# Norms of Q and K by a GpSimd power, in a written order, and idle products at the start of an encoder block

## The chip, the core and the metric

The kernel runs on one core of one Trainium2 chip. The metric is the device time of one execution in microseconds (us). A core has TensorE for matrix products (PE; its weight loads are PEld), VectorE (DVE), ScalarE (ACT), GpSimd (POOL) and SyncE (SP), which issues most of the transfers. Each works through its own instructions in order. Products land in PSUM, in eight banks of 128 x 512 float32; everything else works in SBUF.

## What is computed

One layer of a bidirectional encoder on 1024 tokens of width 1024. The part that matters:

```
u = RMSNorm(x)
[q|k|v|cB|cC|cH|gA|gB] = u @ W_in            # q, k, v: 512 wide each, 8 heads x 64
q = rms_norm(q per head, q_norm_g);  k = rms_norm(k per head, k_norm_g)
y_A = neighbourhood_attention(q, k, v) @ W_A;  y_B = cB * conv3(cC * cH) @ W_B
x = x + (sigmoid(gA) * y_A + sigmoid(gB) * y_B) @ W_o
x = x + relu(RMSNorm(x) @ W1)^2 @ W2
rms_norm(z) = z * rsqrt(mean(z^2) + 1e-6) * g
```

## The kernel before

Every product is made of float16 parts: each operand is scaled by a power of two and split into a high part and a low part, and three passes (high x high, high x low, low x high; `PASSES`, L453) are summed in PSUM. The high part is a ScalarE copy to float16, the low part a VectorE subtraction.

**The start, to V.** Rows come in eight blocks of 128. For blocks 0 and 1, V's columns are multiplied in float32: `native_turn` (L570) transposes the raw rows on TensorE and ScalarE (VectorE for part of block 1) copies them out, `native` (L581) multiplies them by the raw weights. `native(0, 0, lower)` and `native(0, 0, upper)` are two halves of the first product. Meanwhile `largest` and `v_largest` find the largest weight, a matmul with the ones tile (`v_sum`, L546) brings it to all partitions, and `v_part` splits V's weights. The norms of the rows use `rpow` (L417): a scale and a power of -1/2 on GpSimd, on one column per block. The other six blocks go through float16 and transposing DMAs (`ln_turn`) and then through `v_unit` (L528), 24 matmuls of 128x512, in the order 2, 6, 3, 7, 4, 5.

**Weights.** A `Chunk` is one weight matrix piece: `prep` (L255) squares its raw pieces on ScalarE, sums over partitions by a matmul with the ones tile (`all_sum`, L200), derives the scale on VectorE (L426 to L433, L279) and splits it (L306 high, L297 low). These steps are a generator; `push` puts it in the background list and `tick` advances it. `apart(units[0], n)` makes it wait for n further units of TensorE. Five raw buffers are filled by SP as they come free.

**The forms.** Pairs of row blocks (n, n + 4) are scaled (`sform_rows`, ScalarE), combined (`sform_sums`, four GpSimd additions of 128x512), split (L504 ScalarE, L506 VectorE, 128x2048) and stored to DRAM for the gates much later. The foreground generator `sforms` does this at marks counted in units (`SFORM`), and ScalarE issues the stores.

**Q and K.** Sixteen units follow, Q's eight blocks and then K's, each 24 matmuls into one bank of 128 tokens x 512. `unit` (L207) issues the matmuls, runs what is due behind the unit before, and then gives the foreground some steps and the background some ticks. Behind each unit stands a foreground generator `qk_vec` (L711): ScalarE copies the bank out with the scale, squares the copy; VectorE sums per head; `rstd` (L401) takes the square root on ScalarE and refines its reciprocal by five small VectorE steps; VectorE multiplies, ScalarE and VectorE split; `finish_qk` (L740) turns the block by a transposing DMA three units later. Generators of several blocks interleave, one step each per round. Two bank tags, "d" and "o", alternate. After Q the code flushes what the background still has of K's parts, after K what it has of the first convolution's.

**After that** two convolution units (`ch_mms`, 24 matmuls each) run, then attention (L936 onward), in which scores, convolution and softmax are interleaved by a written order; then gates and branches, the output projection, and the MLP, mostly 12-matmul units.

Of the kernel before, what the change touches and what calls it, by code (L numbers as in the profile page):

```python
# [52 lines left out]
def encoder_block(ctx: ExitStack, tc: tile.TileContext, x, weights, cols, gqk, rel, masks, out):  # L53
# [25 lines left out]
    sc = base.tile([128, 516], F32, name="sc")  # L79
    sci = sc.bitcast(I32)  # L80
    area = {"keep": [0, 0, 148], "prep": [148, 148, 244], "tmp": [244, 244, 516]}
# [163 lines left out]
    class Chunk:  # L245
# [9 lines left out]
        def prep(self):  # L255
# [5 lines left out]
            if self.kind in "QKCG":  # L261
                self.parts = wsp.tile([128, 2, tot], F16, name="w16_ws", tag="ws")
                for p, (k, w) in enumerate(self.widths):
                    while len(self.raw) <= p:
                        yield WAIT
                    A.activation(self.parts[:, 1, :k * w].bitcast(BF16), self.raw[p][:, :k * w], AF.Square,
                                 accum_out=sc[:, at(rm, p)])
                    spend(0, 300 + k * w * 7 // 8)
                    yield
                V.tensor_reduce(sc[:, a], sc[:, at(rm, 0, n)], axis=AX, op=OP.add)  # L270
                c = ones_col()
                V.tensor_tensor(c, sc[:, a], sc[:, gm2], op=OP.mult)
# [99 lines left out]
    minus_half = keep()  # L372
# [44 lines left out]
    def rpow(ss, n, y, top):  # L417

        v = tmp()
        G.tensor_scalar(sc[:, v], sc[:, ss], 4.0 ** -top / n, 4.0 ** -top * EPS, op0=OP.mult, op1=OP.add)  # L420
        G.tensor_tensor(sc[:, y], sc[:, v], sc[:, minus_half], op=OP.pow)
        yield
# [55 lines left out]
    turned, formed = set(), [0]  # L478
    SFORM = ((9, 0, 0), (9, 2, 1), (10, 1, 0), (10, 3, 1), (11, 0, 1), (12, 1, 1))

# [5 lines left out]
    def sform_sums(n):  # L486
        z = [xt[:, b, c:c + 512] for b in (n, n + 4) for c in (0, 512)]
        for o, a, b, op in ((3, 2, 3, OP.subtract), (2, 0, 2, OP.subtract),
                            (0, 3, 0, OP.subtract), (1, 1, 0, OP.add)):
            G.tensor_tensor(z[o], z[a], z[b], op=op)  # L490

    def sforms():

        for mark, n, split in SFORM:
            yield from apart(mark, 0)
            pair = xt[:, n:n + 5:4]
            if not split:
                sform_rows(n)
                sform_sums(n)
                continue  # L500
            v = wqk.tile([128, 4, 2, 512], F16, name="s16", bufs=3)
            v4 = v.rearrange("p (b h) w c -> p b h w c", b=2)
            f = pair.rearrange("p b (h c) -> p b h c", h=2)
            A.activation(v4[:, :, :, 0], f, AF.Copy)  # L504
            yield
            V.tensor_tensor(v4[:, :, :, 1], f, v4[:, :, :, 0], op=OP.subtract)  # L506
            fg.append(sform_store(n, v))

    def sform_store(n, v):
        yield from apart(units[0], 1)  # L510
        A.dma_start(GS[:, n], v)
        formed[0] += 1
# [5 lines left out]
    def qk_gain():  # L518
        g = gq[:, 0]
        V.tensor_tensor(g, g, gq[:, 1], op=OP.mult)  # L520
        yield
        yield from gain(g, 11, sgq, isgq)

# [103 lines left out]
    native(0, 0, upper)  # L627
# [65 lines left out]
    fg.append(sforms())  # L693
    for b in 4, 5:
        v_unit(b, 11)
        step(3)
    settle()
    flush()

# [11 lines left out]
    def qk_vec(ps, inv, kind, res):  # L711
        qs = wqk.tile([128, 512], F32, name="qs", bufs=3)
        sq = wqk.tile([128, 512], F32, name="sq", bufs=1)
        A.activation(qs, ps, AF.Copy, scale=sc[:, inv])
        A.activation(sq, qs, AF.Square)
        yield
        ss, y = tmp(8), tmp(8)
        V.tensor_reduce(sc[:, ss], sq.rearrange("p (h d) -> p h d", h=8), axis=AX, op=OP.add)
        yield
        yield from rstd(ss, HD, y, 12 if kind == "q" else 0)  # L720
        if kind == "k":
            V.tensor_scalar(sc[:, y], sc[:, y], sc[:, sgq], None, op0=OP.mult)
            yield
        q3 = qs.rearrange("p (h d) -> p h d", h=8)
        V.tensor_tensor(q3, q3, sc[:, y][:, :, None].to_broadcast([128, 8, HD]), op=OP.mult)
        yield
        if kind == "k":
            V.tensor_tensor(q3, q3, gq[:, 0][:, None, :].to_broadcast([128, 8, HD]), op=OP.mult)
        r = 2 if kind == "q" else 1
        t = wqk.tile([128, 8, 2, r, HD], F16, name=kind + "16", tag="q16")  # L730
        q4 = q3[:, :, None, :].to_broadcast([128, 8, r, HD])
        A.activation(t[:, :, 0], q4, AF.Copy)
        yield
        V.tensor_tensor(t[:, :, 1], q4, t[:, :, 0], op=OP.subtract)
        res.append(t)

    q16 = {}
    todo = [("q", b) for b in ORDER] + [("k", b) for b in range(8)]

    def finish_qk(n):  # L740
        kind, b = todo[n]
        while not q16[n]:
            step()
        dst = QD.rearrange("p a e w t -> p (a e w) t") if kind == "q" else KD
        SP.dma_start_transpose(dst[:, :, b * 128:(b + 1) * 128], q16.pop(n)[0].rearrange("p h w r d -> p (h w r d)"))

    for n, (kind, b) in enumerate(todo):
        ch = cQ if kind == "q" else cK
        if n % 8 == 0:
            push(cK if kind == "q" else cConv[0])  # L750
        ps = bank("do"[n % 2])
        q16[n] = []

        def post(ps=ps, kind=kind, n=n, ch=ch):
            fg.append(qk_vec(ps, ch.inv, kind, q16[n]))
        unit(tok_mms(ps, actU, b, ch, 8, 512, 0), post, 4, 6 if 4 < n < 8 else 3)
        if n == 3:
            forced[0] = True
            while formed[0] < 4:
                step()  # L760
            forced[0] = False
# [8 lines left out]
            SP.dma_start(mk, masks)  # L770
            cneg, cinv = keep(), keep()
            V.tensor_scalar(sc[:, cneg], sc[:, isgq], -(2.0 ** -15), None, op0=OP.mult)
            V.tensor_scalar(sc[:, cinv], sc[:, sgq], 2.0 ** 15, None, op0=OP.mult)
            bias = {0: bias_load(0)}
        if n >= 3:
            finish_qk(n - 3)
        if n in (5, 6):
            bias_make(*bias[0], n - 5)
# [19 lines left out]
    while not q16[15]:  # L798
        step()
    settle()  # L800
    finish_qk(15)
# [1120 lines left out]
```

## Time and profile before

| | us |
|---|---|
| time, median of 3 runs | 1204.14 (1203.29 to 1204.56) |
| the profiled execution | 1205.96 |
| its span, first to last instruction | 1204.2 |
| TensorE busy | 1190.9 (99%) |
| VectorE busy | 929.0 (77%) |
| ScalarE busy | 763.3 (63%) |
| GpSimd busy | 435.1 (36%) |
| first Q unit starts | 55.81 |
| first scores of attention start | 153.53 |

The span is cut into stages by the starts of TensorE's units in the timeline. In a timeline row stand the start, the duration, the engine, the line of the kernel, the operation, the tiles (out<-in), the shapes and how many instructions are merged; in brackets the engine's idle time before it and what ended it. In a row of the groups by line stand the busy time and the mean duration of one instruction in nanoseconds. TensorE's durations are modelled and overlap, so its pace is read from the starts. The granted clock is 1.0 throughout.

### The profile page before, as it was taken

Reading aid. Unit: us, or ns where it says so; the run is one execution under the profiler, and the core shown is the slowest. Engines: PE = TensorE matmul, PEld = TensorE weight load, DVE = VectorE, ACT = ScalarE, POOL = GpSimd, SP = SyncE. Lnnn points to the kernel's source line nnn. Section 1 sums busy time; section 2 is a strip of 40 time slices with the busy share of each in tenths; the row PEclk is TensorE's granted clock in tenths of the full one; section 3 lists DMA queues with packets and bytes.
Section 4 is the critical chain, followed back from the end, with each engine's and each line's share of the span. In section 5 each row is a group of like instructions: output and inputs, shape, how many; then the busy total and the mean of one; then the engine's idle time right before and its main releaser. Section 6 shows DMA issues by size and latency. Waiting matters only on the chain.

```text
span 1204.2 us, 16886 instructions
## 1 busy us (share of the span) xinstructions
PE 1190.9 (99%) x6206; PEld 574.7 (48%) x6206; DVE 929.0 (77%) x1721; ACT 763.3 (63%) x1185; POOL 435.1 (36%) x292
## 2 busy tenths in 40 slices
PE   8999999999999999999999999999999999999998
PEld 6444445555444444444468444444444444444444
DVE  6767988988368686877878655545549999999997
ACT  7876679867554555337779778678676744746440
POOL 1641011222311112001004465565567471554662
PEclk9999999999999999999999999999999999999999
DMA  9956746676451211224286545445465926345302
GB/s 284 220 181 139 139 119 134 130 146 120 106 121 68 64 60 52 70 92 188 53 159 185 183 156 192 151 138 193 147 247 201 355 94 223 124 139 194 105 35 105
DMA packets 177250, 174.91 MB, mean 145 GB/s; under 512 B 137744, under 2 KB 138256, under 8 KB 173072
## 3 DMA queue, kind: packets, MB, share of 16 engines
q1 hardware_dynamic: 176592, 169.65, 49.0%
q10 hardware_dynamic: 576, 4.19, 0.8%
q8 instruction: 48, 0.79, 0.3%
q14 instruction: 34, 0.28, 0.1%
HBM read 102.51 MB, written 37.75 MB: 116 GB/s over the span
## 4 chain that ended last, share of the span: by engine, by line
PE 78%; DVE 5%; issue 1%; SPq 1%; ACT 1%; DMA 0%; DVEq 0%; ACTq 0%
PE ps_d L210 28%; PE ps_s L210 24%; PE ps_o L210 17%; PE ps_d L1017 6%; PE ps_o L994 1%; PE ps_s L937 1%; SPq L1088 1%; DVE P L977 1%; DVE w_s L1141 1%; DVE sz L951 1%; DVE sg L1257 0%; DVE w_ws L297 0%; ACT w_s L1145 0%; DMA uT<-gs 0%; DVE sc L317 0%
## 5 line engine op out<-in xcount | busy, mean ns | idle before, releaser
L210 PEld LDWEIGHTS <-ops 128*128 128x128 f16 x1356 | 132.5, 98 | 157.3
L210 PEld LDWEIGHTS <-w 128*128 128x128 f16 x1368 | 132.9, 98 | 139.4
L1017 PE MATMUL ps_d<-uT,w_ws 128*128 128x512 f16 x528 | 123.7, 379 | 0.1
L210 PE MATMUL ps_d<-ops 128*128 128x512 f16 (+1 forms) x528 | 118.3, 374 | 0.0
L1743 ACT ACTIVATE ops<-hf,sc 128x2048 f16<-128x2048 f32 x26 | 52.0, 2000 | 98.2 <-PE ps_o L210 35.5
L210 PE MATMUL ps_s<-ops 128*128 128x512 f16 x492 | 112.9, 379 | 0.0
L1130 POOL TENSOR_TENSOR tsum<-raw 128x512 f32<-128x512 f32 x28 | 46.3, 1668 | 148.8 <-ACT raw L1116 148.7
L1323 POOL TENSOR_TENSOR as<-as 128x512 f32<-128x512 f32 x56 | 77.5, 1385 | 38.9 <-ACT as L1603 35.6
L210 PEld LDWEIGHTS <-w_s 128*128 128x128 f16 x588 | 56.7, 98 | 69.6 <-DVE w_s L1141 1.5
L210 PEld LDWEIGHTS <-uT 128*128 128x128 f16 x528 | 51.4, 98 | 64.0 <-issue 2.3
L210 PE MATMUL ps_d<-u2x,w 128*128 128x512 f16 (+1 forms) x360 | 80.0, 372 | 0.0
L1017 PEld LDWEIGHTS <-w_ws 128*128 128x128 f16 x528 | 51.2, 98 | 54.5 <-DVE cv L839 0.4
L210 PE MATMUL ps_o<-ops 128*128 128x512 f16 x336 | 77.1, 379 | 0.0
L1745 DVE SCALAR_TENSOR_TENSOR ops<-hf,sc,ops 128x2048 f16<-128x2048 f32 x26 | 73.4, 2822 | 4.3 <-ACT ops L1743 4.2
L210 PE MATMUL ps_o<-u2T,w 128*128 128x512 f16 (+1 forms) x324 | 71.7, 371 | 0.0
L1116 ACT ACTIVATE raw<-raw,sc 128x256 f32<-128x256 f32 x172 | 71.0, 494 | 0.9 <-DMA raw<-in_weights 0.9
L1130 POOL TENSOR_TENSOR gsum<-raw 128x512 f32<-128x512 f32 x14 | 19.0, 1377 | 132.3 <-issue 71.3
L1145 ACT ACTIVATE w<-raw,sc 128x512 f16<-128x512 f32 (+1 forms) x28 | 24.6, 927 | 54.0 <-DVE sc L432 54.0
L210 PE MATMUL ps_s<-u2T,w 128*128 128x512 f16 (+1 forms) x252 | 52.7, 359 | 0.0
L1636 DVE TENSOR_TENSOR as<-ps_d,as 128x512 f32<-128x512 f32 (+1 forms) x14 | 9.4, 672 | 55.7 <-ACT as L1655 53.4
L960 ACT ACTIVATE sz<-sz,sc 128x384 f32<-128x384 f32 (+1 forms) x64 | 37.2, 582 | 22.4 <-DVE sc L951 15.0
L306 ACT ACTIVATE w_ws<-raw,sc 128x512 f16<-128x512 f32 (+2 forms) x72 | 40.8, 637 | 14.2 <-DVE sc L279 14.2
(360 smaller groups left out, 2633.5 us busy)
## 6 DMA issues: line engine op xcount, KB each, us to landing
raw<-in_weights SPq DMA_DIRECT2D x88, 512.0 KB, 5.3
hs<-as SPq DMA_DIRECT2D x16, 1792.0 KB, 8.8
hf<-hs SPq DMA_DIRECT2D x26, 1024.0 KB, 7.4
w2x<-in_weights SPq DMA_DIRECT2D x16, 512.0 KB, 8.6
raw<-in_weights SPq DMA_DIRECT2D x16, 384.0 KB, 3.4
xt<-in_x SPq DMA_DIRECT2D x8, 512.0 KB, 8.1
gs<-s ACTq DMA_DIRECT2D x4, 1024.0 KB, 3.9
x<-in_x SPq DMA_DIRECT2D x8, 512.0 KB, 10.1
```

Source lines behind the costliest of these rows:

```text
L210: T.matmul(ps, l, r, start=a, stop=b)
L306: A.activation(self.parts[:, 0, f + o:f + o + m], self.raw[p][:, o:o + m], AF.Copy, scale=sc[:, c:c + 1])
L937: T.matmul(ps[:, :nb * 128], QD[:, p, e, w, i * 128:(i + 1) * 128], KD[:, 2 * p + e, lo * 128:(lo + nb) * 128], start=w == 0, stop=w == 1)
L951: V.tensor_tensor_reduce(z[:, :d["n"]], d["ps"][:, :d["n"]], bm, sc[:, cneg], 3.0e38, OP.add, OP.min, accum_out=sc[:, d["mx"]])
L960: A.activation(z, z, AF.Exp, scale=-1.0, bias=sc[:, d["mx"]], accum_out=sc[:, d["sm"]])
L1017: T.matmul(ps, l, r, start=a, stop=b)
L1116: A.activation(v, v, AF.Copy, scale=sc[:, at(g, 4 * i + k)])
L1130: G.tensor_tensor(t[:, o], a, b, op=OP.add)
L1145: A.activation(o(0), w, AF.Copy, scale=sc[:, s])
L1323: sub.tensor_tensor(z[o], z[a], z[b], op=op)
L1743: A.activation(P[:, 1, 0], hf, AF.Copy, scale=sc[:, Rs])
L1745: V.scalar_tensor_tensor(P[:, 1, 1], hf, sc[:, Rs], P[:, 1, 0], op0=OP.mult, op1=OP.subtract)
```

## The change

- `idle_products`: 36 products of the ones tile with itself (128 columns) into a bank that nobody reads, ahead of the first transposes, and 10 behind them. `native(0, 0, ...)` is done in one piece, ahead of the second transposes.
- Q and K: `qk_vec` and `rstd` give way to functions that are called in a written order behind each unit (`qk_chain`). ScalarE squares straight from the bank; VectorE sums; GpSimd scales the sums, adds a guard (epsilon over the square of the chunk's scale, bounded) and raises to -1/2, on 128x8; VectorE multiplies the bank by the result. High and low parts of a block stand behind the square and the sum of the next. The gain of K is folded into its factor once (`qk_gain`). The turns go two units later instead of three, the first three together behind unit 4.
- The banks are taken in the order d, s, o, d, s, o, d, s; the split tiles share buffers of two tags.
- The forms: `sforms` gives way to calls at written places; pairs 0 and 2 before the last V unit, 3 behind it, 1 and 0 among the first Q units; SP issues the stores.
- K's chunk may sum after two further units instead of three, and is pushed behind unit 0 instead of before it; the ticks behind each unit are a table. The masks and the first bias are loaded behind unit 5, the bias made behind units 9 and 10 (before: 3, and 5 and 6).

```diff
@@ Chunk.prep
-                yield from apart(units[0], 1 if self.kind == "Q" else 3)
+                yield from apart(units[0], {"Q": 1, "K": 2}.get(self.kind, 3))
@@ 
-    minus_half = keep()
+    minus_half = keep(8)
@@ qk_gain
+        V.tensor_scalar(g, g, sc[:, sgq], None, op0=OP.mult)
@@ the start
+    idle = bank("s")
+    def idle_products(n):
+        for _ in range(n):
+            T.matmul(idle[:, 0:128], ones[:, 0:128], ones[:, 0:128], start=True, stop=True)
+    idle_products(36)
     native_turn(0)
+    idle_products(10)
...
-    native(0, 0, lower)
+    native(0, 0, eight)
...
     native_turn(1)
-    native(0, 0, upper)
     native(1, 0, eight)
@@ V's last units
-    fg.append(sforms())
-    for b in 4, 5:
-        v_unit(b, 11)
-        step(3)
+    v_unit(4, 11)
+    step(3)
+    sform_rows(0)
+    sform_sums(0)
+    sform_split(2)
+    v_unit(5, 11)
+    step(3)
     settle()
     flush()
+    sform_split(3)
+    sform_store(2)
+    drain()
@@ Q and K
-    def qk_vec(ps, inv, kind, res):
...
+    def qk_square(n, ps):
...
+        A.activation(d["sq"], ps, AF.Square)
+    def qk_sum(n):
...
+        V.tensor_reduce(sc[:, d["ss"]], d["sq"].rearrange("p (h d) -> p h d", h=8), axis=AX, op=OP.add)
+    def qk_power(n):
...
+        G.tensor_scalar(sc[:, d["ss"]], sc[:, d["ss"]], 4.0 ** -TOP[kind] / HD, sc[:, guard[kind]],
+                        op0=OP.mult, op1=OP.add)
+        G.tensor_tensor(sc[:, d["y"]], sc[:, d["ss"]], sc[:, minus_half], op=OP.pow)
+    def qk_norm(n):
...
+        V.tensor_tensor(q3, p3, sc[:, d["y"]][:, :, None].to_broadcast([128, 8, HD]), op=OP.mult)
+        if todo[n][0] == "k":
             V.tensor_tensor(q3, q3, gq[:, 0][:, None, :].to_broadcast([128, 8, HD]), op=OP.mult)
...
+    def qk_chain(n, ps):
+        qk_square(n, ps)
+        if n:
+            qk_high(n - 1)
+        qk_sum(n)
+        qk_power(n)
+        if n:
+            qk_low(n - 1)
+        qk_norm(n)
+    ticks = (0, 2, 4, 0, 4, 8, 6, 6, 2, 2, 3, 4, 4, 5, 5, 5)
+    qk_guard("q", cQ.inv)
     for n, (kind, b) in enumerate(todo):
...
+        unit(tok_mms(ps, actU, b, cQ if kind == "q" else cK, 8, 512, 0), lambda n=n, ps=ps: qk_chain(n, ps), 0, 0)
+        if n == 0:
+            sform_rows(1)
+            sform_store(3)
+            sform_split(0)
+            sform_sums(1, (0, 1))
+            push(cK)
+        if n == 1:
+            sform_store(0)
+            sform_sums(1, (2, 3))
         if n == 3:
+            sform_split(1)
+        if n == 4:
+            sform_store(1)
...
+        for m in (0, 1, 2) if n == 4 else (n - 2,) if n > 4 else ():
+            qk_turn(m)
+        tick(ticks[n])
@@ the first convolution
-    first = [bank("o"), bank("o")]
+    first = [bank("o"), bank("s")]
     for half in range(2):
         unit(ch_mms(first[half], actU, half, cConv[0], 8, 384, 0), None, 8, 4)
-        finish_qk(13 + half)
+        if half == 0:
+            qk_high(15)
+            qk_low(15)
+            qk_turn(14)
+            qk_turn(15)
```

In the changed kernel the order on VectorE behind unit n + 1 is: sum of block n, low part of block n - 1, norm of block n. Ahead of block 0's sum stand the splits of pairs 2, 3 and 0; the split of pair 1 stands between the norm of block 2 and the sum of block 3. K's scale and its first two low parts stand behind the norm of block 4, the other six behind that of block 5; the first convolution's scale is finished behind the norm of block 14, followed by its eight low parts. On GpSimd the last two additions for pair 1 stand between the powers of blocks 0 and 1.

More of the change, by code (lines that the diff above doesn't have):

```diff
@@ L737, in encoder_block, with qk_guard @@
[L737 to L740 removed]
+    blocks, guard = {}, {}
+    todo = [("q", b) for b in ORDER] + [("k", b) for b in range(8)]
+    def qk_guard(kind, inv):
+        e, i = keep(), tmp()
+        V.reciprocal(sc[:, i], sc[:, inv])
+        mul(i, i, i)
+        V.tensor_scalar(sc[:, e], sc[:, i], 4.0 ** -TOP[kind] * EPS, 1e37, op0=OP.mult, op1=OP.min)
+        V.tensor_scalar(sc[:, e], sc[:, e], 1e-36, None, op0=OP.max)
+        guard[kind] = e
```

121 lines of the change are left out of this document (47 added, 74 removed).

## Prediction

> **What bounds the kernel now.** The page of the profile comes first, then TensorE's waits, then the start of each of its units in the timeline.
>
> ```profile
> span 1204.2 us, 16886 instructions
> PE 1190.9 (99%) x6206; PEld 574.7 (48%) x6206; DVE 929.0 (77%) x1721; ACT 763.3 (63%) x1185; POOL 435.1 (36%) x292
> ...
> PE ps_o L574 <- DMA xt<-in_x: 4.5, 1, 4.5
> PE ps_d L210 <- DVE w_ws L297: 1.5, 2, 0.9
> PE ps_o L210 <- ACT qs L714: 1.3, 1, 1.3
> PE ps_d L586 <- DMA raw<-in_weights: 0.6, 1, 0.6
> ```
>
> TensorE is busy 1190.9 of 1204.2 us, so only its own waits and slow products can give time back. The waits listed belong to the load of the first rows, to the weights' low parts (L297) and to a bank that ScalarE had not yet copied out (L714). The timeline gives their price. A unit is 24 matmuls of 128x512.
>
> ```profile
> 0.81 0.17 DVE L194 MEMSET ones<- 128x132 bf16 x1 [0.81 <-PEq L1913]
> 4.49 1.94 PE L574 MATMUL ps_o<-identf,xt 128*128 128x128 f32 x8 [4.49 <-DMA xt<-in_x]
> 7.03 3.75 PE L586 MATMUL ps_d<-raw,vT 128*128 128x256 f32 x8 [0.60 <-DMA raw<-in_weights]
> 10.65 1.95 PE L574 MATMUL ps_o<-identf,xt 128*128 128x128 f32 x8
> 14.23 3.62 PE L586 MATMUL ps_s<-raw,vT 128*128 128x256 f32 x16
> 24.70 5.34 PE L210 MATMUL ps_d<-w_v,uT 128*128 128x512 f16 x24
> ...
> 55.81 5.34 PE L210 MATMUL ps_d<-w_ws,uT 128*128 128x512 f16 x24
> 60.99 5.34 PE L210 MATMUL ps_o<-w_ws,uT 128*128 128x512 f16 x24
> 97.28 0.38 PE L210 MATMUL ps_d<-w_ws,uT 128*128 128x512 f16 x1
> 104.49 5.34 PE L210 MATMUL ps_o<-w_ws,uT 128*128 128x512 f16 x24
> 140.77 5.55 PE L210 MATMUL ps_o<-uT,w_ws 128*128 128x512 f16 x24
> 147.65 5.34 PE L210 MATMUL ps_o<-uT,w_ws 128*128 128x512 f16 x24 [1.33 <-ACT qs L714]
> 153.53 0.38 PE L937 MATMUL ps_s<-kD,qD 128*128 128x256 f16 x2
> ```
>
> A unit starts 5.18 us after the one before (60.99 - 55.81). Q's eight units start at 55.81 and K's at 97.28. K's first unit takes 104.49 - 97.28 = 7.21, so 2.03 is stall. The first convolution unit takes 147.65 - 140.77 = 6.88: 1.70 of stall. From there 5.18 would end at 152.83 and the first scores start at 153.53: 0.70 for the sum and its wait. Together **4.4 us**. Besides, the 8 product records at 7.03 take as long (3.75) as the 16 at 14.23 (3.62): the array runs at half its pace there. After 153.53 TensorE hardly waits, so what is won by then should reach the end.
>
> **Part 1, idle products.** 36 once the ones tile is set (0.98), then 10 behind the first transposes. At half pace 128 columns take an estimated quarter of the 0.43 between two 256-column records (7.03 row: 3.4 us for 8), 0.11, so 36 end near 4.9 and the transposes start up to 0.4 later than 4.49. That is hidden: the first real product waits for weights at 7.03 anyway. If the pace has doubled by then, all 16 records of the first product end at about 10.7, where now only its first half is done, and the second transposes take about 1.0 instead of the 1.95 of the row at 10.65 (an estimate by halving). The next product could start at 11.7 instead of 14.23. Next comes V's second largest element:
>
> ```profile
> 16.01 0.16 DVE L609 CAST ones<-sc 128x1 bf16<-128x1 f32 x1
> ...
> 43.59 0.44 DVE L272 TENSOR_TENSOR ones<-sc 128x1 bf16<-128x1 f32 x1
> ```
>
> VectorE and ScalarE start their work on the second rows 0.4 to 0.7 earlier, so that column is ready near 15.5 and its sum holds TensorE 0.3. Two more products of 3.5 give 22.65 for the first V unit: 2.05 early. Four units on, at 43.4, Q's sum needs the column that is ready at 44.03 now; ScalarE's queue before it is full and only 0.44 ahead, so 43.6. **Q starts at 54.1, 1.7 early** (1.3 if part of the first product still runs at half pace).
>
> The Trainium skill (TensorE: Matmul & The Clock Gate, Part 1) has the clock double after one wholly busy window of about 3.4 us whose phase is free. The pause ahead of 7.03 fits with it; by it the products starting at 1 us would raise the pace between 4.5 and 7.9, which is the spread between 1.7 and 1.3.
>
> **Part 2, the chain of a Q or K block.** These rows carry it:
>
> ```profile
> L718 DVE TENSOR_REDUCE sc<-sq 128x8 f32<-128x512 f32 x16 | 10.9, 682 | 0.6 <-ACT sq L715 0.6
> L725 DVE TENSOR_TENSOR qs<-qs,sc 128x512 f32<-128x512 f32 x16 | 10.7, 672 | 0.1
> L734 DVE TENSOR_TENSOR q<-qs,q 128x1024 f16<-128x1024 f32 x8 | 9.8, 1223 | 9.1 <-ACT q L732 9.1
> L734 DVE TENSOR_TENSOR k<-qs,k 128x512 f16<-128x512 f32 x8 | 5.5, 690 | 2.0 <-ACT k L732 1.9
> L732 ACT ACTIVATE q<-qs 128x1024 f16<-128x1024 f32 x8 | 8.4, 1053 | 6.1 <-DMA qD<-q 4.1 <-DVE qs L725 2.0
> L102 DVE TENSOR_TENSOR sc<-sc 128x8 f32<-128x8 f32 x16 | 4.0, 251 | 0.1
> L714 ACT ACTIVATE qs<-ps_d,sc 128x512 f32<-128x512 f32 x8 | 5.4, 670 | 0.0
> L421 POOL TENSOR_TENSOR sc<-sc 128x1 f32<-128x1 f32 x8 | 4.7, 583 | 0.7
> ```
>
> Gone per block: five small VectorE steps (the L102 row is one), the copy from the bank (0.67) and the square root on ScalarE. Added: a scale and a power on GpSimd, on 128x8. The power on one column takes 0.58 on average; on eight it isn't in the trace. Bounds: 0.58, if eight cost like one, and 8 x 0.58 = 4.6, if each costs a whole one. The nearest row is the same operation on one column, so I take **0.58**, and keep the rest as a rival.
>
> The order now is, per block: sum, low part of the block before, norm (VectorE); GpSimd's two run between sum and norm. That they run beside the low part is not to be had:
>
> ```profile
> 26.53 1.28 DVE L447 SCALAR_TENSOR_TENSOR u<-xt,sc,u 128x1024 f16<-128x1024 f32 x1
> 26.94 0.91 POOL L420 TENSOR_SCALAR sc<-sc 128x1 f32<-128x1 f32 x1 [4.28 <-ACT sq L439]
> 28.57 0.19 POOL L420 TENSOR_SCALAR sc<-sc 128x1 f32<-128x1 f32 x1
> ```
>
> The same one-column scale takes 0.91 and ends with VectorE's instruction (27.81) where alone it takes 0.19 (28.57). So the power mostly starts when the low part ends. The Trainium skill (SBUF — State Buffer, "Who interferes with whom") states just this: a VectorE instruction with two SBUF inputs and a GpSimd one that reads SBUF lock each other out for the whole instruction. It speaks against this change: by it the sum is the forecast's, without it each block would be about 0.6 shorter and the sum that of rival 2.
>
> A Q block thus costs 0.68 + 1.23 + 0.13 + 0.58 + 0.04 + 0.67 = 3.3 us (sum, low part, estimated gaps, power, norm), a K block, with 0.69 for the low part and 0.69 for the second factor, 3.5. Both are below 5.18, but the chain starts late:
>
> ```profile
> 67.46 2.76 DVE L506 TENSOR_TENSOR s<-xt,s 128x2048 f16<-128x2048 f32 x1
> 76.01 2.29 DVE L506 TENSOR_TENSOR s<-xt,s 128x2048 f16<-128x2048 f32 x1 [5.79 <-ACT s L504]
> 72.77 1.26 POOL L490 TENSOR_TENSOR xt<-xt 128x512 f32<-128x512 f32 x1
> 49.17 0.14 DVE L204 TENSOR_SCALAR sc<-ps_o 128x1 f32<-128x1 f32 x1
> 50.10 0.23 DVE L279 TENSOR_SCALAR sc<-sc 128x8 f32<-128x8 f32 x1
> 51.12 5.39 DVE L297 SCALAR_TENSOR_TENSOR w_ws<-raw,sc,w_ws 128x512 f16<-128x512 f32 x8 [0.79 <-ACT w_ws L306]
> raw<-in_weights SPq DMA_DIRECT2D x16, 384.0 KB, 3.4
> ```
>
> Three splits of the input's forms still stand ahead of block 0 on VectorE; the third ends at 70.2 now, and I take 70.4. The norms then end at 73.2 (0), 77.7 (1; two of GpSimd's sums of 1.26 stand ahead of its power), 81.3 (2), 86.9 (3; the fourth split, 2.3, stands first), 90.5 (4). K's scale (1.2, from 49.17 to 50.33) follows at 91.7, two of K's eight low parts at 93.75, block 5 at 98.3, and the other six from there to 102.35 (0.67 each). TensorE reaches K at 54.1 + 8 x 5.18 + 0.1 = 95.65 and needs the third low part 1.5 later, at 97.15; it comes at 99.0. With 0.15 more at the eighth: **2.0 of stall, as before**. "K's parts sooner" saves nothing yet.
>
> From 102.35: blocks 6 and 7 end at 105.7 and 109.7, the K blocks 8 to 14 (K's guard, two bias steps and a weight sum among them) at 113.9, 118.25, 122.95, 126.45, 129.95, 133.45 and 138.15, and the convolution's parts start at 138.4. TensorE is there at 102.85 + 7 x 5.18 + 0.1 = 139.1. **The 1.70 goes**, with 0.1 to spare; the second bank is long free. Next late is the sum for the following weights. It waits for block 15's low part, and that for ScalarE, which squares four weight pieces first; the last is loaded once the low parts end at 143.9 and lands 3.4 later (median of its row). With the square, high part, low part and column after it (estimated 0.95 + 0.63 + 0.69 + 0.35) that is 149.9, or a microsecond more if the loads queue, against TensorE at 149.5: 0.5 to 1.6 with the sum, taken 1.1, **0.4 more than now**.
>
> SP now also issues the four stores of the forms and waits for each split, the last near 83.6; the turns of blocks 0 to 2 stand behind it, and their first use as a freed buffer is after 99. The moved loads are hidden likewise.
>
> **Sum**: -1.7 + 0.0 - 1.7 + 0.4 = -3.0 by rows; I take -2.6, since the 0.1 to spare is less than what this reckoning is good for. The profiled execution took 1205.96, with 1204.2 of span; the same 2.6 off the median of 1204.14 gives **1201.5**.
>
> **Rivals.**
> 1. *The power is dearer* (slower). Six powers stand ahead of K's parts and nine more ahead of the convolution's, each on the chain. Every 0.1 us above 0.58 costs 1.5 us. The gain is gone at 0.75 each; at 1.0 the time is 1201.5 + 6.3 = 1207.8; at the upper bound a block would take over 7 us, beyond TensorE's 5.18, and the stage would take some 50 us more. For: nothing shows eight columns at one's price. Against: the one-column scale (0.19) shows that most of a small instruction can be its start.
> 2. *The powers slip in beside the low parts*, or ahead of them, where the block before is normed late. Then five blocks gain 0.4 to 0.6, K's parts come in time, 2.0 more goes: 1199.3. Against: the 0.91 row.
> 3. *The idle products don't raise the pace before the first product ends.* Then the first 1.7 goes and up to 0.4 is lost with the later transposes; the rest stays: 1201.5 + 2.1 = 1203.6.
>
> **How the numbers follow.** Forecast 0.47, rival 1 0.28, rival 2 0.20, rival 3 0.05. A measurement of this kernel tells 0.2%, 2.4 us, from nothing. Of the forecast about half lies beyond that (0.24), with rival 2 (0.20): faster 0.44. Same: the other half of the forecast, rival 3, little of rival 1: 0.29. Slower: 0.27. Range: 1198.3, rival 2 with a microsecond more, to 1211, a power of about 1.2 us; beyond lie 0.05 and 0.14.
>
> **What will show it.** The rows of the first products (about 3.6 for 16 at 7); the first V unit at 22.7 and Q at 54.1; the power's duration, and whether it ends with a low part; K's first unit starting at 95.7 and lasting 7.2; the first convolution unit without stall; the first scores near 150.5. The forecast is wrong first of all if the eight-column power takes over 0.75 us.

## The result, and the profile after

The changed kernel takes 1218.6 us (median of 4 runs, 1217.6 to 1219.8) where the kernel before takes 1204.35 on the same chip (4 runs, 1203.3 to 1205.6). The ratio is 1.0118, with a 95% interval from 1.0101 to 1.0136: it is slower by some 14 us, where 1201.5 was forecast. The profiled execution took 1217.62, with a span of 1215.8, 11.6 more than before; the difference of the medians is larger, because the profiled execution before (1205.96) was slower than those four, and this one is among the faster of its four.

The first rows are the page's head and TensorE's waits in the changed kernel.

```profile
span 1215.8 us, 16907 instructions
PE 1195.2 (98%) x6252; PEld 577.1 (47%) x6252; DVE 924.2 (76%) x1642; ACT 745.9 (61%) x1151; POOL 468.0 (38%) x324
...
PE ps_o L210 <- ACT w_ws L306: 6.4, 1, 6.4
PE ps_d L210 <- DVE w_ws L297: 5.6, 2, 5.1
PE ps_d L210 <- ACT w_ws L306: 1.5, 1, 1.5
```

The wait for the first rows is no longer in the list, and nor is ScalarE's copy of a bank. In their place stand two long waits for weights that are not yet split: 5.1 us for low parts from VectorE (L297), 6.4 for high parts from ScalarE (L306). VectorE and ScalarE are less busy than before, so they are not short of time; they do the splits too late.

The timeline of TensorE says where (start, duration, and in brackets the idle time ahead of it):

```profile
11.62 3.72 PE L577 MATMUL ps_s<-raw,vT 128*128 128x256 f32 x16
22.40 5.34 PE L210 MATMUL ps_d<-w_v,uT 128*128 128x512 f16 x24
...
53.87 5.34 PE L210 MATMUL ps_d<-w_ws,uT 128*128 128x512 f16 x24
97.51 0.38 PE L210 MATMUL ps_d<-w_ws,uT 128*128 128x512 f16 x1 [1.50 <-ACT w_ws L306]
104.91 5.22 PE L210 MATMUL ps_d<-w_ws,uT 128*128 128x512 f16 x17 [5.14 <-DVE w_ws L297]
109.97 5.34 PE L210 MATMUL ps_s<-w_ws,uT 128*128 128x512 f16 x24
152.82 6.68 PE L210 MATMUL ps_o<-uT,w_ws 128*128 128x512 f16 x24 [6.41 <-ACT w_ws L306]
159.34 5.34 PE L210 MATMUL ps_s<-uT,w_ws 128*128 128x512 f16 x24
164.55 0.38 PE L977 MATMUL ps_s<-kD,qD 128*128 128x256 f16 x2
```

Q starts at 53.87, 1.94 sooner than before. K's first unit should begin at 53.87 + 8 x 5.18 = 95.31, and in fact 0.54 later because the sum for K's weights waited for its column; the unit after it starts at 109.97, so K's first unit stalls 109.97 - 95.85 - 5.18 = 8.94 (2.03 before). The first convolution unit should begin at 109.97 + 7 x 5.18 = 146.2 and its second half starts at 159.34: 7.9 of stall (1.70 before). The first scores follow with 0.03 (0.70 before). The sum is -1.94 + 0.54 + 6.91 + 6.2 - 0.67 = **11.0**, and the first scores are in fact 164.55 - 153.53 = 11.02 later. Of the span's 11.6 all but 0.6 has come about by then.

Two rows stand out. The 17 products at 104.91 take 5.22 and the 24 at 152.82 take 6.68, where 24 undisturbed ones take 5.34. In the single records six or seven products behind each long wait start 427 ns apart in place of 216. Two stretches of the profile show the same in the granted clock (the third figure from the end, 1.00 in the stretches around them):

```profile
104.30:107.80 3.50, 2.89 (x7) 0.98 (x7) 3.50 (x6) 1.47 (x2) 0.00 (x0) 0.51 0.99 189
148.70:155.50 6.80, 2.68 (x7) 0.98 (x8) 4.22 (x9) 3.35 (x7) 1.75 (x2) 0.50 0.29 56
```

The second begins during the wait, so only its last 2.7 us cost anything. At the start this figure does not help: in the kernel before it reads 1.00 from 7 to 10 us, where the products run at half pace.

Why VectorE is late is seen in its own rows for the first five blocks: the norms (L749), and behind the fifth the reading of K's sum (L204), with which K's scale begins.

```profile
73.72 0.69 DVE L749 TENSOR_TENSOR qs<-ps_d,sc 128x512 f32<-128x512 f32 x1 [2.16 <-POOL sc L743]
79.28 0.69 DVE L749 TENSOR_TENSOR qs<-ps_s,sc 128x512 f32<-128x512 f32 x1 [1.92 <-POOL sc L743]
83.85 0.69 DVE L749 TENSOR_TENSOR qs<-ps_o,sc 128x512 f32<-128x512 f32 x1 [1.53 <-POOL sc L743]
90.36 0.69 DVE L749 TENSOR_TENSOR qs<-ps_d,sc 128x512 f32<-128x512 f32 x1 [1.89 <-POOL sc L743]
94.93 0.69 DVE L749 TENSOR_TENSOR qs<-ps_s,sc 128x512 f32<-128x512 f32 x1 [1.53 <-POOL sc L743]
95.53 0.15 DVE L204 TENSOR_SCALAR sc<-ps_s 128x1 f32<-128x1 f32 x1
```

Each norm waits 1.5 to 2.2 for GpSimd's power (L743), together 9.0 us. K's sum is read at 95.53 and K's scale is done at 96.70 (L279); the sum was read at 90.46 before, and the forecast had the scale done at 91.7. The two instructions on GpSimd, with the shortest, median and longest duration in ns:

```profile
L741 POOL TENSOR_SCALAR sc<-sc x16: 271/635/1171, 71.7 to 157.8; 128x8 f32<-128x8 f32 x16
L743 POOL TENSOR_TENSOR sc<-sc x16: 1637/1639/2674, 72.0 to 158.5; 128x8 f32<-128x8 f32 x16
L421 POOL TENSOR_TENSOR sc<-sc x8: 548/556/685, 13.7 to 33.3; 128x1 f32<-128x1 f32 x8
```

The power on eight columns takes 1.64 us where that on one column takes 0.55. The scale, which rose only from 0.19 to 0.27 for eight columns, and the power do not grow alike.

### The profile page after: what moved, and what is told of

The parts are those of the page before. It is cut to its first block, busy times and chain, and to the rows that moved or that the text cites. A ratio compares the mean times of both kernels' runs of the same rounds, so it can differ in the third digit from the quotient of the medians.

```text
span 1215.8 us, 16907 instructions
## 1 busy us (share of the span) xinstructions
PE 1195.2 (98%) x6252; PEld 577.1 (47%) x6252; DVE 924.2 (76%) x1642; ACT 745.9 (61%) x1151; POOL 468.0 (38%) x324
## 4 chain that ended last, share of the span: by engine, by line
PE 77%; DVE 11%; ACT 5%; POOL 4%; issue 2%; DMA 0%; SPq 0%; DVEq 0%; ACTq 0%; POOLq 0%
PE ps_d L210 25%; PE ps_s L210 23%; PE ps_o L210 17%; PE ps_d L1057 9%; POOL sc L743 2%; DVE w_s L1181 2%; PE ps_s L977 2%; PE ps_o L1034 1%; DVE s L498 1%; POOL sc L741 1%; DVE sg L1297 1%; DVE sc L737 1%; ACT w_ws L306 1%; DVE qs L749 1%; ACT sq L439 1%
## 5 line engine op out<-in xcount | busy, mean ns | idle before, releaser
L1057 PEld LDWEIGHTS <-w_ws 128*128 128x128 f16 x528 | 51.3, 98 | 54.1
L1170 POOL TENSOR_TENSOR gsum<-raw 128x512 f32<-128x512 f32 x14 | 19.0, 1376 | 132.6 <-issue 53.6
L306 ACT ACTIVATE w_ws<-raw,sc 128x512 f16<-128x512 f32 (+2 forms) x72 | 40.7, 636 | 27.0 <-DVE sc L279 27.0
## 6 DMA issues: line engine op xcount, KB each, us to landing
x<-in_x SPq DMA_DIRECT2D x8, 512.0 KB, 10.9
```

The source lines that it names most:

```text
L306: A.activation(self.parts[:, 0, f + o:f + o + m], self.raw[p][:, o:o + m], AF.Copy, scale=sc[:, c:c + 1])
L1057: T.matmul(ps, l, r, start=a, stop=b)
L1170: G.tensor_tensor(t[:, o], a, b, op=OP.add)
```

## The experiments

Twelve builds ran, those with the same figure in the column `before` on one chip, with runs of the kernel before beside them. Medians in us:

```
kernel                              this      before    ratio [95%]
before + idle products              1204.11   1205.38   0.9990 [0.9981, 0.9999]
changed, no idle products           1215.98   1205.38   1.0091 [1.0078, 1.0105]
changed, power on 1 column          1202.75   1205.38   0.9969 [0.9956, 0.9983]
before + powers of many widths      1204.38   1205.38   one run
changed, norm one chain later       1209.07   1204.46   1.0033 [1.0021, 1.0044]
changed, power on 4 columns         1207.22   1204.46   1.0021 [1.0012, 1.0030]
changed, products in both waits     1216.26   1204.46   1.0093 [1.0079, 1.0107]
changed, again                      1218.20   1204.46   1.0114 [1.0098, 1.0129]
norm two chains later               1203.13   1205.10   0.9980 [0.9972, 0.9989]
the same, no idle products          1201.38   1205.10   0.9967 [0.9955, 0.9980]
the same, tail moved, no idle       1199.97   1204.56   0.9961 [0.9948, 0.9975]
tail moved, with idle products      1201.25   1204.56   0.9969 [0.9957, 0.9980]
```

What the experiments have to tell apart: **T**, that the power costs 1.64 in place of 0.58 and each tenth of that is paid on VectorE's chain; against **R**, that the written order itself puts K's scale and the splits too late, whatever the power costs. Besides: what the idle products are worth.

### The power on one column

```
- G.tensor_tensor(sc[:, d["y"]], sc[:, d["ss"]], sc[:, minus_half], op=OP.pow)
+ G.tensor_tensor(sc[:, at(d["y"], 0)], sc[:, at(d["ss"], 0)], sc[:, at(minus_half, 0)], op=OP.pow)
- ... sc[:, d["y"]][:, :, None].to_broadcast([128, 8, HD])
+ ... sc[:, at(d["y"], 0)][:, :, None].to_broadcast([128, 8, HD])
```

> The changed kernel with the power taken on one of the eight columns, and every head multiplied by that one (part of the norm is left out); all else stands as it is. Theory T (the eight-column power, 1.64 us, stands on the chain from a block's sum to its norm): power 0.55, six powers fewer us ahead of K's parts, K's first unit with 1 to 2.5 us of stall, none at the first convolution unit, time 1201 to 1203. Rival R (the written order puts K's and the convolution's scale too late whatever the power costs, or the stores on SP hold the queue): both stalls stay over 5 us, time over 1212.

1202.75, 2.6 below the kernel before on the same chip, where the changed kernel stands 13.7 and 14.3 above it: some 16.5 us go with 1.09 of power, 1.5 for each tenth, and R falls. (The kernel leaves out seven of the eight norms; apart from the power's width its instructions take as long as before.) The rows of the power, of VectorE's norm ahead of K's sum, and of TensorE at K's first unit:

```profile
L743 POOL TENSOR_TENSOR sc<-sc x16: 547/548/1583, 72.1 to 144.2; 128x1 f32<-128x1 f32 x16
...
89.47 0.69 DVE L749 TENSOR_TENSOR qs<-ps_s,sc 128x512 f32<-128x512 f32 x1 [0.44 <-POOL sc L743]
90.08 0.15 DVE L204 TENSOR_SCALAR sc<-ps_s 128x1 f32<-128x1 f32 x1
98.36 3.90 PE L210 MATMUL ps_d<-w_ws,uT 128*128 128x512 f16 x17 [1.33 <-DVE w_ws L297]
```

The norm's wait falls from 1.53 to 0.44, K's sum is read 5.45 sooner, which is five powers at 1.09. Both chains now stand where the forecast had them: the sum is read at 90.08 (forecast 90.5), and the convolution's low parts begin at 138.43 (forecast 138.4). The convolution's first unit starts at 138.45, with 0.3 of stall in all. The same 17 products that took 5.22 now take 3.90: behind a wait of 1.3 us there is no half pace. In this profile the first scores start at 149.07, 4.46 sooner than in the kernel before, while the span is only 2.0 shorter; more on that below.

### Powers of many widths

Twelve instructions on GpSimd's scratch columns while it was idle, behind the kernel before's own work at unit 6.

```
+ for op in (OP.pow, OP.mult):
+     for c in (1, 2, 4, 8, 16, 32):
+         G.tensor_tensor(pw[:, 2, 0:c], pw[:, 0, 0:c], pw[:, 1, 0:c], op=op)
```

> The kernel before with twelve instructions more on GpSimd where it idles (behind the second bias, near 106 us): a power and then a product on 1, 2, 4, 8, 16 and 32 columns of a scratch tile. T: the power costs by the column, about 0.40 + 0.155 for each: 0.55, 0.7, 1.0, 1.64, 2.9, 5.4; products near 0.1 to 0.2 up to 32 columns. Rival (the 1.64 comes from VectorE's instructions in its way): under 0.8 at 8 columns. Time as before.

The timeline of GpSimd, powers of four widths and one product:

```profile
104.79 0.55 POOL L785 TENSOR_TENSOR pw<-pw 128x1 f32<-128x1 f32 x1
106.20 1.01 POOL L785 TENSOR_TENSOR pw<-pw 128x4 f32<-128x4 f32 x1
107.30 1.64 POOL L785 TENSOR_TENSOR pw<-pw 128x8 f32<-128x8 f32 x1
109.01 2.90 POOL L785 TENSOR_TENSOR pw<-pw 128x16 f32<-128x16 f32 x1
...
118.87 0.20 POOL L785 TENSOR_TENSOR pw<-pw 128x8 f32<-128x8 f32 x1
```

A power costs 0.39 to start and 0.156 for each column: 0.55, 0.71, 1.01, 1.64, 2.90. A product on the same eight columns takes 0.20, and between one and eight columns products rise only from 0.19 to 0.20. Two of the twelve are far off the expectation, the 32-column power (5.98 for 5.4) and the 16-column product (0.54, where 32 columns take 0.28); both began while VectorE ran an instruction with two SBUF inputs. The forecast's error thus stands by itself: eight columns of a power were priced like one, and against a dearer power spoke only a row of a cheaper operation, which says nothing of how this one grows.

### The power on four columns

```
- G.tensor_tensor(sc[:, d["y"]], sc[:, d["ss"]], sc[:, minus_half], op=OP.pow)
+ G.tensor_tensor(sc[:, at(d["y"], 0, 4)], sc[:, at(d["ss"], 0, 4)], sc[:, at(minus_half, 0, 4)], op=OP.pow)
... (the norm multiplies heads 4 to 7 by the norms of heads 0 to 3)
```

> The changed kernel with the power on four of the eight columns; heads 4 to 7 are multiplied by the norms of heads 0 to 3, that part of the norms is left out. The power alone should take 1.01 us (the measured row for four columns). Theory T (each 0.1 us of power costs 1.5 us of time, along the whole way from 0.55 to 1.64): 1202.8 + 4.6 x 1.5 = 1209.5, 1208 to 1211; stalls of K's and the convolution's first products some 2.5 to 3 us below the changed kernel's 8.9 and 7.9 each. Rival R (only a power longer than the slack of a period costs, so the time jumps between 1.0 and 1.64): 1202 to 1205.

1207.2, between the two expectations. Against the kernel before on the same chip it is +2.8, where one column has -2.6 and eight +13.7: from one to four columns 5.4 us for 0.46 (1.2 for each tenth), from four to eight 10.9 for 0.63 (1.7). So 1.5 for each tenth is only the mean of a bent line. TensorE's rows show the bend:

```profile
101.01 5.51 PE L210 MATMUL ps_d<-w_ws,uT 128*128 128x512 f16 x17 [3.59 <-DVE w_ws L297]
143.39 5.58 PE L210 MATMUL ps_o<-uT,w_ws 128*128 128x512 f16 x24 [0.58 <-ACT w_ws L306]
```

K's first unit stalls 5.4 (1.6 with one column, 8.9 with eight), the convolution's 1.0 (0.3 and 7.9). The six powers ahead of K's parts are paid at once, from the start also with the half pace behind a wait of 3.6. The nine that follow have cover: from the first K block's norm to the seventh's (L749) the norms start 4.4 apart on average with the power of 1.01 and 5.1 apart with 1.64, against TensorE's 5.18, so VectorE makes up for the delay until the convolution in the one case and hardly in the other.

### Products in the two waits, and the changed kernel again

```
+ (in words) 22 products of 128x512, from UT into the next unit's bank, behind the 7th of K's first unit
+ for _ in range(26):
+     T.matmul(first[0], UT[:, 0, 0, 0:128], UT[:, 0, 0, 0:512], start=True, stop=True)
  for half in range(2):
      unit(ch_mms(first[half], actU, half, cConv[0], 8, 384, 0), None, 8, 4)
```

> The changed kernel, with 22 products of 128x512 into a bank not in use put where K's first unit waits 5.1 us, and 26 where the convolution's first unit waits 6.4 us; nothing else. Theory P (after PE has stood for 5 to 6 us the next six or seven products run at half pace, 427 ns from start to start in place of 213, whatever caused the wait): the first products after both places run at 213 ns, and 2.6 us go: ratio to the kernel before lower by 0.002 than the changed kernel's in this call, 1216.0. Rival R (what follows is late for its own reasons, so the pace of the first products hides nothing): no change, within 0.5 us; or the slow products stay, and the pace was not from the wait.

> The changed kernel as it is, for comparison in this call: ratio to the kernel before 1.0118 as first measured, within 0.0015; both theories expect the same.

1216.26 against 1218.20: 1.9 less, as theory P had it (the intervals of the ratios overlap, so the rows must carry it). First the kernel with the products, then the changed kernel again:

```profile
104.46 3.90 PE L210 MATMUL ps_d<-w_ws,uT 128*128 128x512 f16 x17 [0.40 <-DVE w_ws L297]
152.34 5.57 PE L210 MATMUL ps_o<-uT,w_ws 128*128 128x512 f16 x24 [2.08 <-ACT w_ws L306]
```

```profile
103.87 6.71 PE L210 MATMUL ps_d<-w_ws,uT 128*128 128x512 f16 x17 [5.15 <-DVE w_ws L297]
151.85 8.14 PE L210 MATMUL ps_o<-uT,w_ws 128*128 128x512 f16 x24 [4.98 <-ACT w_ws L306]
```

With TensorE kept busy, the 17 products take 3.90 and the 24 take 5.57; without, 5.22 and 6.68 in the first profile and 6.71 and 8.14 in this one, where 12 and 13 products in a row ran at half pace. The granted clock is 1.00 from 97 to 110 us and from 144 to 158 in the kernel with the products, and 0.50 from 102.9 to 109.7 and from 150.7 to 157.5 in this profile of the changed kernel. So the half pace comes from standing still, and it is part of the price of a long wait: 1.1 to 2.8 us each here. Whether it makes the spread of the changed kernel's times is open, since the four runs without it still differ by 2.0. And what is saved is not all paid out: the convolution's weights come at 152.34, against 152.82 and 151.85 without the products, so its first unit still stalls 8.1.

The Trainium skill (TensorE: Matmul & The Clock Gate, Part 1) says that one idle window of about 3.4 us takes the array back to half its clock. The waits of 3.6, 5.1 and 6.4 agree. In the next kernel the granted clock falls at two waits of 2.0 as well, one of them with 0.36 more close behind, which are shorter than that.

### The norm one chain later

```
  qk_square(n, ps)
- if n:
-     qk_high(n - 1)
  qk_sum(n)
  qk_power(n)
- if n:
-     qk_low(n - 1)
- qk_norm(n)
+ if n > 1:
+     qk_low(n - 2)
+ if n:
+     qk_norm(n - 1)
+     qk_high(n - 1)
... (each turn one block later, the last blocks finished behind the convolution's first half)
```

> The changed kernel with each block's norm put one chain later: VectorE's order is sum of n, low part of n-2, norm of n-1, so that the eight-column power of n runs beside other blocks' work and nothing on VectorE waits for it; transposes one block later. Theory T (the power's 1.64 us stood fifteen times in a chain PE ends up waiting for): the first scores come as early as with the one-column power, about 149 in the profile, no wait over 2 us at K's or the convolution's first product; 1200 to 1203 us, below the kernel before. Rival R (it is the chain's order and length, not the power: a block has more work on VectorE and GpSimd than PE gives it time): K's first unit still waits over 3 us and the time is above 1210.

1209.07: neither. Behind the first block no norm waits for a power any more, yet K's sum is read only at 91.48, and TensorE shows

```profile
98.89 1.47 PE L210 MATMUL ps_d<-w_ws,uT 128*128 128x512 f16 x6 [2.01 <-DVE w_ws L297]
100.72 3.97 PE L210 MATMUL ps_d<-w_ws,uT 128*128 128x512 f16 x11 [0.36 <-DVE w_ws L297]
154.33 0.16 PE L201 MATMUL ps_d<-ones 128*128 128x1 bf16 x1 [2.02 <-DVE ones L272]
154.65 2.97 PE L1060 MATMUL ps_d<-uT,w_ws 128*128 128x512 f16 x7
```

K's first unit still stalls 4.1. The half pace is there again: behind the first wait of 2.0 us six products still run at full pace (1.47), but of the eleven behind the next 0.36 seven start 427 ns apart (granted clock 0.51 from 100.2 to 103.6); behind the second wait of 2.0 seven products take 2.97 (1.67 undisturbed; granted clock 0.50 from 154.9 to 158.2). ScalarE's queue shows why K is late: the high part of a block stands in it ahead of the next block's square, and now waits for the norm.

```profile
87.57 1.06 ACT L758 ACTIVATE q<-qs 128x1024 f16<-128x1024 f32 x1 [4.21 <-DVE qs L749]
88.54 0.58 ACT L732 ACTIVATE sq<-ps_s 128x512 f32<-128x512 f32 x1
91.60 1.06 ACT L758 ACTIVATE q<-qs 128x1024 f16<-128x1024 f32 x1 [2.48 <-DVE qs L749]
```

Square, sum, low part, norm and high part are one loop of 4.0 us again (87.57 to 91.60). The theory was too narrow: with the power out of the loop, another loop through two engines was left, and it too catches up too slowly with the late start of the chain.

### The norm two chains later, and with or without idle products

```
  qk_square(n, ps)
- if n:
-     qk_high(n - 1)
+ if n > 1:
+     qk_norm(n - 2)
+     qk_high(n - 2)
  qk_sum(n)
  qk_power(n)
- if n:
-     qk_low(n - 1)
- qk_norm(n)
+ if n > 1:
+     qk_low(n - 2)
... (each turn one block later, the last two blocks finished behind the convolution's first half)
```

> The changed kernel with each norm two chains later and first in its chain: VectorE's order is norm of n-2, sum of n, low part of n-2; ScalarE's square of n, high part of n-2. Neither a power of 2.8 us with its scaling nor ScalarE's wait for the norm stands in the loop from one block to the next, which is norm 0.69, high part 1.06 and low part 1.22, some 3.3 us against PE's 5.18. Theory T (the loop of a block, with the power or, in the version with the norm one chain later, with ScalarE's 2.5 us wait for the norm, made VectorE late for K's scale and the parts): K's sum is read before 90.1, K's and the convolution's first products wait under 2 us, first scores at 148 to 150, time 1199.5 to 1202.5. Rival R (the written order itself puts the scale and the parts late, whatever the loop): K's sum read at 91 or later, 1206 to 1210 as with one chain.

> The same without the idle products and with the first product in halves. Theory S (idle products are worth what the start of Q's products gains, 1.3 to 1.9 us, where nothing later is late): 1.3 to 1.9 us above the version with them. Rival (the gain of the start is swallowed by K's or the convolution's parts, which are placed by the other engines): within 0.6 us of it.

1203.13 with idle products, below the kernel before by 0.2%, though above the 1202.5 that T allowed. The rows (VectorE, GpSimd, TensorE):

```profile
85.55 0.15 DVE L204 TENSOR_SCALAR sc<-ps_s 128x1 f32<-128x1 f32 x1
L743 POOL TENSOR_TENSOR sc<-sc x16: 1638/1642/2523, 71.1 to 141.5; 128x8 f32<-128x8 f32 x16
94.92 5.34 PE L210 MATMUL ps_d<-w_ws,uT 128*128 128x512 f16 x24
100.10 5.34 PE L210 MATMUL ps_s<-w_ws,uT 128*128 128x512 f16 x24
136.39 5.34 PE L210 MATMUL ps_o<-uT,w_ws 128*128 128x512 f16 x24
148.54 0.16 PE L201 MATMUL ps_d<-ones 128*128 128x1 bf16 x1 [1.63 <-DVE ones L272]
```

The powers are as long as in the changed kernel, the order of the stages is the same, and both stalls are nil: K's first unit takes 5.18, the convolution's too. K's sum is read at 85.55, ten microseconds sooner. So it was the power's place in the loop, together with ScalarE's wait for the norm, and R falls a second time. What is left is the 1.6 ahead of the scores.

Without idle products it takes 1201.38, 1.75 less and not 1.3 to 1.9 more: theory S missed, and so did its rival, which allowed 0.6. The two profiled executions (1202.70 without, 1202.31 with) don't show this difference, so its cause stays open.

### The last block behind the convolution's second half

```
(in words)
- for m in 14, 15: norm, high, low; turns      (all behind the first half)
+ norm, high, low and turn of 14 + half        (one block behind each half)
```

> The version with the norm two chains later and without idle products, with the norm and the parts of the last block put behind the convolution's second half, so that VectorE reaches the column of the next weights' sum before PE. Theory T (PE's 1.6 us wait for that column, just ahead of the first scores, was VectorE's tail): the wait is under 0.3 us, first scores 1.4 to 1.7 us sooner than 150.2; time 1199.7 to 1201.2. Rival R (what is gained before the scores is taken back at 630 to 660 us, where PE waits for VectorE and for transfers): 1201.0 to 1202.

> The same with the idle products and the undivided first product. Theory S (idle products are worth the 1.5 us by which Q's products start sooner): 1.0 to 1.8 us below the version without them in this call. Rival R (the stretch at 630 to 660 us takes it back, and the start's own wait for the weights changes from execution to execution): within 0.6 us of it, or above it as in the pair before.

1199.97 without idle products, ratio 0.9961 [0.9948, 0.9975]: this version beats both kernels, by 4.6 and some 18 us. Its longest wait and its first scores:

```profile
PE ps_o L565 <- DMA xt<-in_x: 4.4, 1, 4.4
...
147.47 0.38 PE L971 MATMUL ps_s<-kD,qD 128*128 128x256 f16 x2
```

The 1.6 is gone (the next longest wait is 0.5), and the scores start 6.1 sooner than in the kernel before. With idle products it takes 1201.25: no gain from them here either, so S missed twice.

### What the idle products are worth

```
+ idle = bank("s"); 36 idle products, native_turn(0), 10 idle products
- native(0, 0, lower) ... native(0, 0, upper)
+ native(0, 0, eight)
```

This was added to the kernel before, and the reverse was done to the changed kernel.

> The kernel before with the idle products and the undivided first product alone. Both theories: the first Q unit starts near 53.9, 1.9 us early. Theory S1 (what the start wins reaches the end): about 1202.4, 1.9 less than before. Theory S2 (VectorE's work on the forms and on Q starts only 0.5 us earlier, so K's first unit waits the longer): about 1203.8, K's first unit with 3.4 us of stall instead of 2.0.

> The changed kernel without the idle products and with the first product in two halves again. S1: 1.9 us over the changed kernel, 1220.5. S2: 0.6 over it, 1219.2, with K's and the convolution's parts at about the same place and 1.3 less stall ahead of K's first unit's end.

Added to the kernel before they save 1.27 (ratio 0.9981 to 0.9999), between the two expectations: in that profile Q starts 1.7 sooner, the scores 2.5, K's first unit stalls 2.8 and the convolution's 0.15. The gain is not all the pace's, then. Taking them out of the changed kernel costs nothing: 1215.98, 10.6 above the kernel before on its chip, against 13.7 to 14.3 with them, where 0.6 to 1.9 more was expected. Both expectations missed, though the intervals (1.0078 to 1.0105, and 1.0098 to 1.0136) overlap, so that a gain from taking them out isn't shown either. The start of Q's units in the profiles (us from the start of the span):

```
with idle products      52.8  53.5  53.7  53.8  53.9  53.9  54.1  54.3  54.5     mean 53.8
without                 53.6  53.7  54.1  55.0  55.8                             mean 54.5
```

The kernel before's own profile, from which the forecast was made, is the 55.8. VectorE could read its first weights only at 6.92, the latest of all profiles (5.70 at the soonest). TensorE waited 0.6 for them there and not at all in the other four without idle products, and was still at half pace in the second transposes (1.95 there, 1.07 or 1.08 in the four). With idle products the start hardly depends on that as far as V: its first unit starts at 21.7 to 22.4, without them at 22.2 to 24.7. But in five of the nine TensorE then waits 0.3 to 0.9 for transposed rows (uT), so on Q's start the mean gain is 0.6, not 1.7, and the two groups overlap. In the written order not even that counts as long as TensorE waits for VectorE: VectorE's chain starts with the last split of the forms ahead of block 0, and that stands 54.3 behind GpSimd's first norm of the rows in all eleven profiles of that order (13.47 to 67.77 in the changed kernel, 12.03 to 66.36 without idle products), whenever Q starts.

## Why the prediction was wrong, point by point

- **The price of the power: the step that failed.** "The nearest row is the same operation on one column, so I take 0.58": it is 1.64 on eight. The bounds of 0.58 and 4.6 held it, the choice did not. The row that was to speak against a dear power was that of the scale, an operation whose eight columns cost hardly more than one; the power has a cost for each column. With the power at one column's price the rest of the chain came out as forecast (K's sum at 90.08 for 90.5, the convolution's parts at 138.43 for 138.4).
- **Rival 1, "the power is dearer"**, names the mechanism, and its price of 1.5 us for each tenth gives 1201.5 + 10.6 x 1.5 = 1217.4 at 1.64, against 1218.6. The one-column kernel shows it (some 16.5 for 1.09). That it comes so near is partly luck: its line is not straight (1.2, then 1.7 for each tenth), and some 2.5 of the 11 us in the profile are half pace behind waits, which no step had. The range ended at a power of 1.2, well inside the bounds that the prediction itself gave; that cut is why it missed.
- **K's first unit, "2.0 of stall, as before":** 8.9. With the power at one column's price 1.6, so the step was right for its own premise; K's scale was to be done at 91.7 and was done at 96.7, five powers later, and at 91.2 with one column.
- **The convolution's first unit, "the 1.70 goes":** 7.9; with one column 0.3.
- **The sum ahead of the scores, 0.4 more:** 0.7 less. Here the step was wrong by itself: the convolution is so late that the sum is ready, but with one column, where it is in time, the scores follow just as closely (143.86 + 5.18 = 149.04, scores at 149.07). In the two kernels with the norm two chains later the sum is late by 1.6.
- **The start, Q at 54.1:** 53.87, right to 0.25, with the second product at 11.62 for 11.7 and the first V unit at 22.40 for 22.65. But the 1.7 was measured against an execution with an unusually late start; on the mean it is 0.6. The pace did rise before the first product, so rival 3 falls: all 16 records at 6.97 take 3.69.
- **Rival 2, powers beside the low parts:** it does not happen. The rows of a low part and of a power begun with it:

```profile
92.17 1.23 DVE L762 TENSOR_TENSOR q<-qs,q 128x1024 f16<-128x1024 f32 x1 [0.41 <-ACT q L758]
92.22 2.67 POOL L743 TENSOR_TENSOR sc<-sc 128x8 f32<-128x8 f32 x1
88.69 1.64 POOL L743 TENSOR_TENSOR sc<-sc 128x8 f32<-128x8 f32 x1
```

  The low part ends at 93.40, the power at 94.89, 1.49 later: of its 1.64 only 0.15 was done beside it. The trace agrees with the rule that the prediction weighed (the Trainium skill, SBUF — State Buffer, "Who interferes with whom").
- **"What is won by then should reach the end":** not always. With one column 4.5 us were won at the first scores and 2.0 at the end. The other 2.5 go in three waits of TensorE between the scores and 660 us that the kernel before does not have (0.4, 0.7 and 1.4). The longest comes about at 631 to 659 us, where ScalarE waits for a weight load, VectorE for ScalarE, and TensorE for VectorE:

```profile
641.31 3.30 ACT L1156 ACTIVATE raw<-raw,sc 128x256 f32<-128x256 f32 x8 [2.72 <-DMA raw<-in_weights]
659.26 2.75 PE L210 MATMUL ps_s<-u2T,w 128*128 128x512 f16 x12 [1.40 <-DVE as L1685]
```

  The load is issued behind two transposing transfers that land 7.6 and 7.1 after their issue there, and 6.9 and 5.5 in the kernel before. The 1.4 occurs in three profiles (one column, norm two chains later, tail moved with idle products), all with idle products; in the others this wait is 0.9 or less, without idle products 0.4 or less. So the kernel with the norm two chains later, whose scores start 1.5 sooner with idle products than without, loses 1.0 of that here. In the last pair the profile with idle products started Q 0.4 later than the one without, so there was no earlier start to lose. Why these transfers take longer in some executions was not tried and stays open.
- **Two sums** of the prediction are slightly off and decide nothing: 102.85 + 7 x 5.18 + 0.1 is 139.2, not 139.1, and rival 2's "2.0 more goes" gives 1199.5, not 1199.3.

## What to carry to other kernels

A price taken over from another width is only as good as the knowledge whether the operation costs by its start or by its elements: where the bounds lie a factor of eight apart and the operation stands fifteen times in a loop, the range must reach to where the dear end leads. Such an operation on a slow engine needed no cheaper form here once its consumer was moved two steps down the loop, so that no queue held an instruction which waited for it; one step was not enough, because the wait moved to the other engine's queue. A gain at the start of a kernel is to be taken against several executions, not against the profiled one.

## What the runs showed of the hardware

- GpSimd's power on 128 partitions takes 0.39 us and 0.156 for each column (0.55, 0.71, 1.01, 1.64, 2.90 for 1, 2, 4, 8, 16); its product takes 0.19 to 0.20 for 1 to 8.
- Around waits of TensorE of 3.6 and of 5.0 to 6.4 us, and around two of 2.0 (one with 0.36 more close behind), the granted clock was 0.5 for 3.4 or 6.8 us, and six to thirteen products of 128x512 started 427 ns apart in place of 216, which cost 1.1 to 2.8 us each time. It began during the wait or up to six products behind it. At waits of 1.3 and 1.6 the clock stayed at 1.00, and at one of 2.1 that followed 26 products into a bank not in use.
- In the 14 profiles the first weights could be read at 5.7 to 6.9 us, and Q's first unit started at 52.8 to 54.5 with idle products and at 53.6 to 55.8 without. The two don't go together from one profile to the next: without idle products weights at 5.70 went with Q at 54.15, and weights at 6.32 with Q at 53.63.
